# Block 2 projects the delta rule's keys and gates first, then the attention's queries and keys; the substitution is written between them

## The chip, the cores and the metric

The kernel runs on one core of one Trainium2 chip. The metric is device time in microseconds (us) of one execution; the time before is the median of three runs. A profile of one further execution tells what each engine did: TensorE (PE in the rows; PEld is its weight load), VectorE (DVE), ScalarE (ACT), GpSimd (POOL) and the queue that issues most transfers (SP).

## The reference

Two transformer blocks over one sequence of 512 tokens, 1024 channels, in float32. Block 1 (attention, pooling, a gated MLP) is not touched. Block 2 mixes tokens in two ways and then runs a mixture of experts:

```python
h = rms_norm(x, ln1_g)
proj = h @ w_in                      # 3*512 + 4*512 + 16 columns
aq, ak, av, dqkv, dz, dab = jnp.split(proj, ...)
aq = rms_norm(hs(aq), q_norm_g)      # 8 heads of 64
ak = rms_norm(hs(ak), k_norm_g)
attn = rms_norm(neighbourhood_attention(aq, ak, hs(av), rpb), attn_out_g)
dn = bidirectional_gated_deltanet(dqkv, dz, dab[:, :, 0], dab[:, :, 1], ...)
x = x + jnp.concatenate([attn, dn], axis=-1) @ w_out
x = x + hierarchical_moe(rms_norm(x, ln2_g), ...)
```

The delta net puts queries, keys and values through a convolution of width 5 and a SiLU, normalises queries and keys, and solves a unit lower triangular system per head, direction and chunk; its matrix is `beta * k k^T * decay`, so it needs the keys and the gates (from the 16 columns `dab`), but neither queries nor values:

```python
lower = jnp.where(strict, jnp.einsum('bhnid,bhnjd->bhnij', kb, k) * decay, 0.0)
a_mat = jnp.eye(c, dtype=f32) + lower
sol = lax.linalg.triangular_solve(a_mat, rhs, left_side=True, lower=True, unit_diagonal=True)
```

## The kernel before

Activations lie transposed, channels on partitions and the 512 tokens along the free dimension, in eight tiles. Every float32 product is made of three matmuls of rounded halves (`mm3`, lines 177 to 179): the weights are split by `split_w` into `whi` (ACT, line 170) and `wlo` (DVE, line 171) after their load into one of three `wraw` buffers, the activations into `hh` and `hl`.

Block 2's input is projected in chunks of 256 columns. `proj` makes 48 matmuls of 128x512 into two PSUM buffers `pj0` and `pj1`; the tag `mm` has two buffers, so a projection begins a buffer only when the last one's has been emptied. There are two chunks each of the attention's queries (`na_q`; in this text q0 and q1), its keys (k0, k1) and values (`na_v`; v0, v1), and of the delta rule's keys (`dn_k`), queries (`dn_q`), values (`dn_v`) and output gate (`dn_z`). `na_v` puts tokens on partitions: four groups of 24 matmuls 128x272 or 128x256 into one PSUM buffer each; v0 also has the 16 columns `dab` of the delta rule's gates. ACT empties these groups with a scale `rr` per token (line 792). `rr` is the reciprocal norm: column sums of the squares (line 311), a power on POOL (line 670), two products on DVE. The projections themselves run on unnormalised activations, and `RR`, its broadcast (line 351), is multiplied in by POOL at the convs (line 870).

`head_norm` follows q and k: ACT copies and squares the two PSUM buffers (lines 732 and 735), PE sums the squares (`hn`, 738), DVE scales (742, 743), POOL raises to the power -1/2 (745, two instructions on the tile `hnv`), DVE multiplies by `rr` (746). `head_rows` transposes the result on PE (`hr`, 753) and sends it through DRAM; `head_bcast` loads it back over partitions, and `na_q_out` and `na_k_out` multiply (772, 777; tiles `zq`, `akp`).

`conv_silu` follows the delta rule's q, k and v: ACT empties PSUM (869), POOL multiplies by `RR` (870), ACT starts and DVE adds four taps (871, 875), ACT makes the tanh (877), DVE the end (878). `gates` (900 to 928) makes the decays from `dab`. `dn_k_out` makes, per head, a transpose of the keys (`ktr`, 964), their square sums (968), `kk` = k k^T (984), and per direction the decay (`E`, 950 and 951) and `U` (990); one direction is transposed (996). Blocks of 32x32 of `U` go to DRAM (998) and come back as `LB` (1001), 128 blocks on 128 partitions. `substitute` inverts these blocks: for m from 31 to 1 a product (`TB`, 1019) and a sum (`XB`, 1021) over the columns above; DVE has columns 24 to 31 (31 steps), POOL those below 24 (23 steps). Its results go to DRAM (1025) and are used by `levels`, the stage behind the projections. `x_rows` (700) writes the normalised residual as rows, and the bias tables `bm` of the neighbourhood attention are made by POOL (812).

The order of work is not written engine by engine: except for one block of attention code with a schedule by hand, the framework's scheduler orders each engine's instructions when the program is built, from the written order, the dependencies and the number of buffers. Each engine then takes its instructions in that order. The written order of block 2's calls is what the change edits (lines 1211 to 1246, before).

Of the kernel before, what the change touches and what calls it, by code (L numbers as in the profile page):

```python
# [89 lines left out]
def hybrid_kernel(ctx, tc, A, out, dbg=None):  # L90
# [20 lines left out]
    def V(name, i=0, n=1):  # L111
        o, _ = _VEC[name]
        return vec[:, o + i:o + i + n]
# [42 lines left out]
    def split_w(src, n=8, into=None, w=256):  # L156

        his, los = [], []
        g = 1024 // w
        for k in range(0, n, g):  # L160
            m = min(g, n - k)

            def part(tag, dt):
                t = wp.tile([128, 1024], dt, tag=tag, name=tag, bufs=3)
                return t[:, :m * w].rearrange("p (m w) -> p m w", m=m)

            raw = into[k // 4] if into else part("wraw", F32)
            nc.sync.dma_start(raw, src[:, k:k + m, :])
            hi, lo = part("whi", F32R), part("wlo", F32R)
            nc.scalar.activation(hi, raw, AF.Copy)  # L170
            nc.vector.tensor_tensor(lo, raw, hi.bitcast(F32), op=ALU.subtract)  # L171
            his += [hi[:, i, :] for i in range(m)]
            los += [lo[:, i, :] for i in range(m)]
        return his, los
# [478 lines left out]

    w_first = split_w(A["win2"][0])
    nc.vector.tensor_tensor(gs[:, 8:16], V("fg", 0, 8), V("ln1", 0, 8), op=ALU.mult)
    hh, hl = new_h()
    for j in range(8):
# [66 lines left out]
    def head_norm(pp, gain):  # L726

        pt = ps("pa", "hn")
        aa = []
        for m in range(2):  # L730
            a = slot("cv", "a", 6)
            nc.scalar.activation(a, pp[m], AF.Copy, scale=gain)
            aa.append(a)
            sq = slot("cv", "sq", 6)
            nc.scalar.activation(sq, pp[m], AF.Square)
            for t in range(4):
                o = m * 8 + t * 2
                nc.tensor.matmul(pt[:, o:o + 2], sq[:, t * 128:t * 128 + 128], C("hsel"), start=True, stop=True)
        v, r = (sp_.tile([128, 2] + d, F32, tag=f"hn{i}", name="hnv", bufs=1 + i) for i, d in enumerate(([4, 2], [2, 4])))
        pv = pt[:, 0:16].rearrange("p (m t e) -> p m t e", m=2, t=4)  # L740
        for m in range(2):
            nc.vector.tensor_tensor(v[:, m], pv[:, m], rr2.unsqueeze(2).to_broadcast([128, 4, 2]), op=ALU.mult)
        nc.vector.tensor_scalar(v, v, 1.0 / 64, EPS, op0=ALU.mult, op1=ALU.add)
        for m in range(2):
            nc.gpsimd.tensor_tensor(v[:, m], v[:, m], nhalf.rearrange("p (t e) -> p t e", t=4), op=ALU.pow)
            nc.vector.tensor_tensor(r[:, m].rearrange("p e t -> p t e"), v[:, m], rr.unsqueeze(2).to_broadcast([128, 4, 2]),
                                    op=ALU.mult)
        return aa, r
# [15 lines left out]
        return R  # L764

    def na_q(c):
        return head_norm(proj(A["win2"][c] if c else w_first, hh, hl), g8)

    def na_q_out(c, aa, r):
        for m in range(2):  # L770
            R = head_bcast(r, m)
            nc.vector.tensor_tensor(unperm(zq[2 * c + m]), perm(aa[m]), perm(R), op=ALU.mult)
# [7 lines left out]

    def na_v(c):
        w = 256 if c else 272
        hi, lo = split_w(A["win2"][5] if c else A["win2v"], w=w)
        for i in range(4):
            p = ps("mm", "pv")
            ts = slice(i * 128, i * 128 + 128)
            for k in range(8):
                mm3(p[:, 0:w], hh[k][:, ts], hl[k][:, ts], hi[k], lo[k], k, k == 0, k == 7)
            if not c:
                nc.vector.tensor_scalar(dab[:, i, :], p[:, 256:272], rr[:, i:i + 1], None, op0=ALU.mult)  # L790
            v = slot("nP", "vn", 4, (128, 256))
            nc.scalar.activation(v, p[:, 0:256], AF.Copy, scale=rr[:, i:i + 1])
            nc.sync.dma_start(vscr[c][ts], v)
        src = vscr[c].rearrange("(r b x) w -> b r x w", r=8, b=8)
        for b in range(8):
            i, o = (b + 1) // 2, 64 * ((b + 1) % 2)
            nc.sync.dma_start(vsh[i][o:o + 64, c * 256:c * 256 + 256], src[b])
# [410 lines left out]
            new_mix2(4 + h)  # L1208
            split_h(mixh[4 + h], mixl[4 + h], da[h])

    q_ = na_q(0)
    x_rows(2)
    pk = proj(A["win2"][2], hh, hl)
    x_rows(0)
    k_ = head_norm(pk, V("kg"))
    q_ = head_rows(*q_)
    na_v(0)
    x_rows(3)
    x_rows(1)
    na_q_out(0, *q_)  # L1220
    rst.close()
    bp2 = st.enter_context(tc.tile_pool(name="blk2b", bufs=1))
    LB = slot("Z", "LB", 2, (128, 32, 32))
    XB = slot("Z", "XB", 2, (128, 32, 32))
    dn_k(0)
    gates()
    k_ = head_rows(*k_)
    dn_k(1)
    na_k_out(0, *k_)
    dn_k_out(0)  # L1230
    q2_ = na_q(1)
    pk2 = proj(A["win2"][3], hh, hl)
    dn_k_out(1)
    q2_ = head_rows(*q2_)
    na_q_out(1, *q2_)
    k2_ = head_norm(pk2, V("kg"))
    k2_ = head_rows(*k2_)
    na_k_out(1, *k2_)
    dn_q(1)
    dn_q(0)  # L1240
    na_v(1)
    substitute()
    dn_q_out(0)
    dn_v(1)
    dn_v(0)
# [679 lines left out]
```

## Time and profile before

| what | value |
|---|---|
| runs | 1555.94, 1557.53, 1548.36 us; median 1555.94 |
| profiled execution | 1553.21 us, span 1551.3 us |
| mean granted TensorE clock | 0.972 of full speed |
| instructions | 20448 |
| busy, share of the span | PE 95%, PEld 65%, DVE 54%, ACT 33%, POOL 16% |
| block 2's projections | about 613 to 845 us of the span |

The span runs from the first to the last instruction; the profiled execution's own time is 1.9 us above it. A row of the waits names what an engine waited for last; a timeline row gives start and duration, and in brackets the idle time of that engine just before it with what ended it. Matmuls are pipelined, so that the starts of two neighbours, and not the duration of one, give the rate. PEclk is the granted clock of TensorE, where 1.00 is its 2.4 GHz level and 0.50 the 1.2 GHz level.

### The profile page before, as it was taken

To read this page: it belongs to the slowest core of one execution; us is meant where nothing else is said; L and a number is where in the kernel's file an instruction comes from. 1 tells how busy PE (TensorE), PEld (TensorE's weight loads), DVE (VectorE), ACT (ScalarE), POOL (GpSimd) and SP (SyncE) were. 2 spreads that over 40 slices of the span, in tenths; PEclk is the share of its full clock that TensorE was granted. 3 is DMA by queue.
4 is the path that set the end of the run, shared out by engine and by line. 5 is a ranking of instruction groups with operands and counts; after the bars stand their busy time and mean duration, and the time that the engine had idled before them with its cause. 6 is when DMAs were issued, how large, how long until landed. Compare 5 with 4: busy or idle time off the path is not lost.

```text
span 1551.3 us, 20448 instructions
## 1 busy us (share of the span) xinstructions
PE 1467.0 (95%) x7500; PEld 1012.8 (65%) x7500; DVE 842.6 (54%) x1724; ACT 516.1 (33%) x981; POOL 251.6 (16%) x317
## 2 busy tenths in 40 slices
PE   6899999999999999998889999997999999999997
PEld 3766686888888887876667788884444444444443
DVE  3778776653564457266797666564333333233234
ACT  4554434441442345254334434422311111111111
POOL 0242021000000004323562330102100000000000
PEclk9989999999999999998989999997999999999999
DMA  8753143332222223353333131567999999999995
GB/s 334 244 201 122 60 145 109 103 101 94 96 96 95 95 82 99 101 171 102 85 116 77 30 92 50 196 220 295 421 418 424 425 423 424 424 424 424 423 424 185
DMA packets 82573, 327.69 MB, mean 211 GB/s; under 512 B 18086, under 2 KB 21798, under 8 KB 58144
## 3 DMA queue, kind: packets, MB, share of 16 engines
q1 hardware_dynamic: 80736, 321.63, 55.4%
q0 software_dynamic: 1728, 4.66, 0.8%
q8 instruction: 61, 1.00, 0.3%
q14 instruction: 48, 0.39, 0.1%
HBM read 319.42 MB, written 8.47 MB: 211 GB/s over the span
## 4 chain that ended last, share of the span: by engine, by line
PE 76%; DVE 10%; DMA 4%; issue 3%; POOL 3%; ACT 2%; SPq 1%; DVEq 0%; POOLq 0%; ACTq 0%
PE pgu L1728 14%; PE pj L177 10%; PE pj L179 10%; PE pj L178 10%; PE pd L1757 7%; PE pkept L1775 2%; PE pkept L1776 2%; PE pcmb L1775 2%; PE pcmb L1776 2%; DVE wlo L171 2%; DMA graw<-in_modw_dram 1%; DVE cv L875 1%; PE pS L485 1%; DMA xg<-xs,tok_of 1%; DVE E L950 1%
## 5 line engine op out<-in xcount | busy, mean ns | idle before, releaser
L177 PE MATMUL pj<-hh,whi 128*128 128x512 f32 x640 | 259.2, 406 | 16.1 <-ACT cn L869 7.7
L179 PE MATMUL pj<-hh,wlo 128*128 128x512 f32 x640 | 257.2, 403 | 4.8 <-DVE wlo L171 4.8
L178 PE MATMUL pj<-hl,whi 128*128 128x512 f32 x640 | 257.1, 402 | 0.5 <-DVE hl L200 0.5
L1728 PE MATMUL pgu<-wgu,xw 128*64 128x512 f32 x1024 | 227.1, 596 | 0.1
L171 DVE TENSOR_TENSOR wlo<-wraw,whi 128x1024 fp32r<-128x1024 f32 (+4 forms) x122 | 148.4, 1218 | 47.6 <-ACT whi L170 44.5
L170 ACT ACTIVATE whi<-wraw 128x1024 fp32r<-128x1024 f32 (+4 forms) x122 | 125.0, 1027 | 136.3 <-PE pj L178 119.2
L1728 PEld LDWEIGHTS pgu<-wgu,xw 128*64 128x64 f32 x1024 | 70.4, 137 | 139.3 <-issue 137.9
L177 PEld LDWEIGHTS pj<-hh,whi 128*128 128x128 f32 x640 | 123.5, 193 | 48.8 <-ACT cn L869 10.2
L179 PEld LDWEIGHTS pj<-hh,wlo 128*128 128x128 f32 x640 | 123.7, 194 | 34.6 <-DVE wlo L171 5.3
L178 PEld LDWEIGHTS pj<-hl,whi 128*128 128x128 f32 x640 | 123.8, 193 | 26.0 <-issue 1.2
L1734 DVE SCALAR_TENSOR_TENSOR hid<-pgu,agt,sg 128x256 f32<-128x256 f32 x32 | 15.5, 484 | 194.0 <-ACT sg L1732 194.0
L1732 ACT ACTIVATE sg<-pgu,agt 128x256 f32<-128x256 f32 x32 | 15.2, 476 | 305.1 <-PE pgu L1728 305.1
L1757 PE MATMUL pd<-wd,hT 128*64 128x512 f32 x512 | 115.5, 593 | 0.4 <-ACT xgT L1580 0.4
L1779 DVE TENSOR_TENSOR xr<-xr,pcmb 128x512 f32<-128x512 f32 x128 | 82.2, 683 | 28.7 <-PE pcmb L1776 28.7
L306 POOL TENSOR_TENSOR acc<-acc,sq 128x512 f32<-128x512 f32 x21 | 33.7, 1623 | 391.6 <-ACT sq L305 391.3
L198 DVE SCALAR_TENSOR_TENSOR og<-pd,agt,og 128x512 fp32r<-128x512 f32 x64 | 48.0, 750 | 79.6 <-ACT og L194 79.6
L1719 POOL COPY xw<-xgT 128x512 f32 x56 | 32.9, 616 | 353.8 <-PE pgu L1728 343.7
L1757 PEld LDWEIGHTS pd<-wd,hT 128*64 128x64 f32 x512 | 36.2, 137 | 72.3 <-issue 63.1
L179 PE MATMUL pj<-ah,wlo 128*128 128x512 f32 x176 | 69.3, 394 | 0.0
L177 PE MATMUL pj<-ah,whi 128*128 128x512 f32 x176 | 69.3, 394 | 0.0
L178 PE MATMUL pj<-al,whi 128*128 128x512 f32 x176 | 69.3, 394 | 0.0
L194 ACT ACTIVATE og<-pd,agt 128x512 fp32r<-128x512 f32 x64 | 44.0, 688 | 75.3 <-PE pd L1757 74.2
(455 smaller groups left out, 2630.3 us busy)
## 6 DMA issues: line engine op xcount, KB each, us to landing
wgu<-in_egu_dram SPq DMA_DIRECT2D x128, 1024.0 KB
wd<-in_ed_dram SPq DMA_DIRECT2D x62, 1024.0 KB
graw<-in_modw_dram SPq DMA_DIRECT2D x48, 512.0 KB
wraw<-in_wup_dram SPq DMA_DIRECT2D x42, 512.0 KB
wraw<-in_win_dram SPq DMA_DIRECT2D x38, 512.0 KB
wraw<-in_wdn_dram SPq DMA_DIRECT2D x20, 512.0 KB
wraw<-in_wout_dram SPq DMA_DIRECT2D x16, 512.0 KB
E<-gscr SPq DMA_DIRECT2D x16, 256.0 KB
```

The lines of the kernel that those rows point to most:

```text
L170: nc.scalar.activation(hi, raw, AF.Copy)
L171: nc.vector.tensor_tensor(lo, raw, hi.bitcast(F32), op=ALU.subtract)
L177: nc.tensor.matmul(p, whi, hh, start=first, stop=False)
L178: nc.tensor.matmul(p, whi, hl, start=False, stop=False)
L179: nc.tensor.matmul(p, wlo, hh, start=False, stop=last)
L194: nc.scalar.activation(hi, src, AF.Identity, scale=scale, bias=0.0 if bias is None else bias)
L198: nc.vector.scalar_tensor_tensor(lo, src, scale, hi.bitcast(F32), op0=ALU.mult, op1=ALU.subtract)
L1728: nc.tensor.matmul(gu[64 * i:64 * i + 64, :], xw[:, j, 64 * i:64 * i + 64], wts.gu[e][j], start=(j == 0), stop=(j == 7))
L1757: nc.tensor.matmul(pd[64 * i:64 * i + 64, :], hT[:, j, 64 * i:64 * i + 64], wts.d[e][:, j, n * 512:n * 512 + 512], start=(j == 0), stop=(j ...
L1775: nc.tensor.matmul(pc, OT[:, ts], a, start=(n == 1 or start), stop=False, skip_group_check=(n == 0))
L1776: nc.tensor.matmul(pc, OT[:, ts], b, start=False, stop=(n == 1 or stop), skip_group_check=(n == 0))
L1779: nc.vector.tensor_tensor(v, v, pc, op=ALU.add)
```

## The change

The calls of block 2 are written in another order; no instruction's work is altered. Values v0 with the gate columns come first (so the weights that are split while block 1 ends are `win2v`, not the first query chunk), then both halves of the delta rule's keys, the gates and `dn_k_out`, interleaved with q0 and k0, then q1 and k1. `substitute()` is written behind `head_rows` of q1, ahead of `head_norm` of k1, where it stood behind `dn_q` and v1. `na_v(1)` now stands ahead of `dn_q`.

```diff
-    w_first = split_w(A["win2"][0])
+    w_first = split_w(A["win2v"], w=272)
...
     def na_q(c):
-        return head_norm(proj(A["win2"][c] if c else w_first, hh, hl), g8)
+        return head_norm(proj(A["win2"][c], hh, hl), g8)
...
-        hi, lo = split_w(A["win2"][5] if c else A["win2v"], w=w)
+        hi, lo = split_w(A["win2"][5], w=w) if c else w_first
...
-    q_ = na_q(0)
+
+    na_v(0)
     x_rows(2)
-    pk = proj(A["win2"][2], hh, hl)
     x_rows(0)
-    k_ = head_norm(pk, V("kg"))
-    q_ = head_rows(*q_)
-    na_v(0)
+    dn_k(0)
     x_rows(3)
     x_rows(1)
-    na_q_out(0, *q_)
     rst.close()
     bp2 = st.enter_context(tc.tile_pool(name="blk2b", bufs=1))
     LB = slot("Z", "LB", 2, (128, 32, 32))
     XB = slot("Z", "XB", 2, (128, 32, 32))
-    dn_k(0)
     gates()
+    dn_k(1)
+    dn_k_out(0)
+    q_ = na_q(0)
+    dn_k_out(1)
+    pk = proj(A["win2"][2], hh, hl)
+    q_ = head_rows(*q_)
+    k_ = head_norm(pk, V("kg"))
+    na_q_out(0, *q_)
     k_ = head_rows(*k_)
-    dn_k(1)
+    q2_ = na_q(1)
     na_k_out(0, *k_)
-    dn_k_out(0)
-    q2_ = na_q(1)
     pk2 = proj(A["win2"][3], hh, hl)
-    dn_k_out(1)
     q2_ = head_rows(*q2_)
+    substitute()
     na_q_out(1, *q2_)
     k2_ = head_norm(pk2, V("kg"))
     k2_ = head_rows(*k2_)
     na_k_out(1, *k2_)
+    na_v(1)
     dn_q(1)
     dn_q(0)
-    na_v(1)
-    substitute()
     dn_q_out(0)
```

On POOL, before, the powers of the head norms of q1 (`hnv_5783`) and k1 (`hnv_6017`) stand among the work on the keys of the delta rule, and the first step of the substitution comes behind all of it (19 rows behind the first power):

```order
L745 TENSOR_TENSOR hnv_5783<-hnv_5783,nhalf_68 128x8 x2
L1011 MEMSET XB_5349 128x32
L973 TENSOR_TENSOR rk_4924<-ka_5652,nhalf_68 128x4
L745 TENSOR_TENSOR hnv_6017<-hnv_6017,nhalf_68 128x8 x2
L1090 MEMSET U_5675 32x4x32 x4
L1090 MEMSET U_5692 32x4x32 x4
L973 TENSOR_TENSOR rk_4924<-ka_5868,nhalf_68 128x4
L870 TENSOR_TENSOR cn_6103<-cn_6103,RR_4861 128x512
L1090 MEMSET U_5891 32x4x32 x3
```

After the change, POOL has the twelfth step (the last one with `12x12`) ahead of the power of q1's head norm, here `hnv_5907`:

```order
L1021 TENSOR_TENSOR XB_5243<-XB_5243,TB_5992 128x13x11
L1019 TENSOR_TENSOR TB_5992<-LB_5242,XB_5243 128x144
L1021 TENSOR_TENSOR XB_5243<-XB_5243,TB_5992 128x12x12
L745 TENSOR_TENSOR hnv_5907<-hnv_5907,nhalf_68 128x8 x2
L1019 TENSOR_TENSOR TB_5992<-LB_5242,XB_5243 128x143
L1021 TENSOR_TENSOR XB_5243<-XB_5243,TB_5992 128x11x13
```

and the last steps of the substitution ahead of that of k1's, here `hnv_6136`:

```order
L1021 TENSOR_TENSOR XB_5243<-XB_5243,TB_5992 128x2x22
L1019 TENSOR_TENSOR TB_5992<-LB_5242,XB_5243 128x23
L1021 TENSOR_TENSOR XB_5243<-XB_5243,TB_5992 128x23
L745 TENSOR_TENSOR hnv_6136<-hnv_6136,nhalf_68 128x8 x2
L870 TENSOR_TENSOR cn_6354<-cn_6354,RR_4867 128x512
L812 TENSOR_TENSOR bm_7185<-masks_4885,rb_7183 128x256
```

Both powers moved from ahead of the substitution's first step to behind its twelfth and its last.

On PE, before, the transpose `hr_5986` of q1's head norm follows the last matmuls of k1 (`pj1_5805`), and behind it come the square sums of k1 (`hn_6000`) and the delta rule's queries (`pj0_6052`):

```order
L178 MATMUL pj1_5805<-hl_4819,whi_5800 128x512
L179 MATMUL pj1_5805<-hh_4811,wlo_5801 128x512
L753 MATMUL hr_5986<-cst_64,hnv_5784 16x128
L738 MATMUL hn_6000<-cst2_4877,sq_6003 128x2 x4
L177 MATMUL pj0_6052<-hh_4804,whi_6042 128x512
L178 MATMUL pj0_6052<-hl_4812,whi_6042 128x512
```

After, it also follows k1 (`pj1_5937`), but reads `hnv_5908`, which DVE makes from POOL's `hnv_5907`; behind it stands v1 (`pv_6171`):

```order
L178 MATMUL pj1_5937<-hl_4825,whi_5932 128x512
L179 MATMUL pj1_5937<-hh_4817,wlo_5933 128x512
L753 MATMUL hr_5986<-cst_64,hnv_5908 16x128
L738 MATMUL hn_6119<-cst2_4883,sq_6122 128x2 x4
L177 MATMUL pv_6171<-whi_6161,hh_4810 128x256
L178 MATMUL pv_6171<-wlo_6162,hh_4810 128x256
L179 MATMUL pv_6171<-whi_6161,hl_4818 128x256
```

and 22 matmuls of v1 later the transpose `hr_6145` of k1's head norm, ahead of the rest of v1:

```order
L179 MATMUL pv_6171<-whi_6167,hl_4824 128x256
L177 MATMUL pv_6171<-whi_6167,hh_4817 128x256
L753 MATMUL hr_6145<-cst_64,hnv_6137 16x128
L178 MATMUL pv_6171<-wlo_6168,hh_4817 128x256
L179 MATMUL pv_6171<-whi_6167,hl_4825 128x256
L177 MATMUL pv_6199<-whi_6161,hh_4810 128x256
```

So the queue behind the first transpose is now v1 in place of the delta rule's queries, and the second transpose stands inside v1.

On DVE after the change the two products of line 746 (`hnv_5908`, which wait for POOL) stand between DVE's own steps of the substitution, and the low halves of v1's weights (`wlo_6162`) behind them:

```order
L742 TENSOR_TENSOR hnv_5907<-hn_5890,rr2_4853 128x8
L772 TENSOR_TENSOR zq_4892<-a_5571,hR_5818 128x8x8x8
L742 TENSOR_TENSOR hnv_5907<-hn_5890,rr2_4853 128x8
L1019 TENSOR_TENSOR TB_5992<-LB_5242,XB_5243 128x156
L743 TENSOR_SCALAR hnv_5907<-hnv_5907 128x16
L1021 TENSOR_TENSOR XB_5243<-XB_5243,TB_5992 128x26x6
L746 TENSOR_TENSOR hnv_5908<-hnv_5907,rr_4852 128x4x2 x2
L1019 TENSOR_TENSOR TB_5992<-LB_5242,XB_5243 128x175
L1021 TENSOR_TENSOR XB_5243<-XB_5243,TB_5992 128x25x7
L1019 TENSOR_TENSOR TB_5992<-LB_5242,XB_5243 128x192
L1021 TENSOR_TENSOR XB_5243<-XB_5243,TB_5992 128x24x8
L1019 TENSOR_TENSOR TB_5992<-LB_5242,XB_5243 128x184
L171 TENSOR_TENSOR wlo_6162<-wraw_6159,whi_6161 128x1024
```

In before the corresponding products stand ahead of the first step.

## Rows read from the trace of the kernel before

**Rows 1.** Head of the page: span, and each engine's busy time, share and instructions.

```profile
span 1551.3 us, 20448 instructions
...
PE 1467.0 (95%) x7500; PEld 1012.8 (65%) x7500; DVE 842.6 (54%) x1724; ACT 516.1 (33%) x981; POOL 251.6 (16%) x317
```

**Rows 2.** Table by stretches: us, length, busy us (count) of PE, PEld, DVE, ACT, POOL; PEclk, DMA, GB/s.

```profile
706.50:720.20 13.70, 11.32 (x37) 9.67 (x38) 8.05 (x22) 5.26 (x11) 5.04 (x11) 0.50 0.32 80
...
745.00:785.00 40.00, 30.62 (x174) 24.97 (x173) 32.03 (x72) 16.64 (x32) 24.61 (x48) 0.96 0.33 90
785.00:845.00 60.00, 53.13 (x237) 41.99 (x237) 50.87 (x116) 24.29 (x50) 22.78 (x31) 0.91 0.33 91
...
806.00:845.00 39.00, 35.80 (x171) 28.49 (x172) 30.63 (x68) 16.81 (x39) 7.94 (x8) 1.00 0.31 76
...
1060.00:1551.00 491.00, 479.97 (x2216) 218.29 (x2216) 170.30 (x281) 82.92 (x177) 42.65 (x66) 0.99 0.96 397
```

**Rows 3.** PE's waits from 600 to 860 us: us in total, times, longest us.

```profile
PE pj L177 <- ACT cn L869: 7.7, 5, 4.5
PE hn L738 <- ACT sq L735: 5.7, 2, 5.2
...
PE hr L753 <- DVE hnv L746: 1.6, 1, 1.6
```

**Rows 4.** Timeline of PE: start us, us, engine, line, operation, out<-in, count, idle before.

```profile
628.87 0.65 PE L351 MATMUL rb<-cst,rr 128*128 128x128 f32 x4
...
634.15 0.71 PE L700 MATMUL xtr<-cst,xT 128*128 128x128 f32 x5
...
649.79 0.37 PE L177 MATMUL pv<-whi,hh 128*128 128x272 f32 x1
...
663.99 1.04 PE L700 MATMUL xtr<-cst,xT 128*128 128x128 f32 x8
...
689.82 0.60 PE L964 MATMUL ktr<-cst,kT 128*128 128x128 f32 x4
...
708.88 1.87 PE L738 MATMUL hn<-cst,sq 128*128 128x2 f32 x8 [5.20 <-ACT sq L735]
...
745.44 0.50 PE L177 MATMUL pj<-hh,whi 128*128 128x512 f32 x1
...
806.24 0.50 PE L177 MATMUL pj<-hh,whi 128*128 128x512 f32 x1 [0.38 <-ACT cn L869]
...
844.42 0.60 PE L1058 MATMUL vtr<-cst,vT 128*128 128x128 f32 x4
```

**Rows 5.** Timeline of POOL, same columns.

```profile
691.87 3.99 POOL L812 TENSOR_TENSOR bm<-masks,rb 128x256 f32<-128x256 f32 x3
...
717.64 3.25 POOL L745 TENSOR_TENSOR hnv<-hnv,nhalf 128x8 f32<-128x8 f32 x2
...
766.93 0.24 POOL L1019 TENSOR_TENSOR TB<-LB,XB 128x23 f32<-128x23 f32 x1
...
771.56 0.40 POOL L1019 TENSOR_TENSOR TB<-LB,XB 128x95 f32<-128x95 f32 x1
...
782.70 0.81 POOL L1021 TENSOR_TENSOR XB<-XB,TB 128x144 f32<-128x144 f32 x1
...
791.79 1.22 POOL L1019 TENSOR_TENSOR TB<-LB,XB 128x95 f32<-128x95 f32 x1
...
797.51 0.24 POOL L1021 TENSOR_TENSOR XB<-XB,TB 128x23 f32<-128x23 f32 x1
```

**Rows 6.** Timelines of ACT, PE and DVE (twice), same columns.

```profile
707.13 0.63 ACT L951 ACTIVATE E<-E 128x512 f32<-128x512 f32 x1 [3.19 <-DVE E L950]
...
749.00 1.08 PE L984 MATMUL kk<-kT 128*128 128x128 f32 x8
...
760.07 0.70 DVE L996 STREAM_TRANSPOSE uT<-U 128x512 f32<-128x512 f32 x1
...
791.38 1.41 DVE L171 TENSOR_TENSOR wlo<-wraw,whi 128x1024 fp32r<-128x1024 f32 x1
```

## The prediction

> **What bounds the kernel now.** I read the head of the page first [rows 1]: TensorE (PE) is busy 1467.0 of 1551.3 us, so time is lost only where PE stops. The table by stretches [rows 2] shows where. From 1060 us on (the experts) PE is busy 479.97 of 491 us beside a DMA share of 0.96; that stage keeps its length and begins when block 2 ends, so a shift of block 2 passes whole to the span. In block 2's projections PE stops: busy 30.62 of 40 us from 745 to 785 and 53.13 of 60 from 785 to 845. PE's waits from 600 to 860 us [rows 3] name the releasers: evicted conv inputs (7.7 us), the squares of a head norm (5.7), a head norm's result (1.6). A stop also costs clock: after the 5.20 us stop at 703.68, 13.7 us run at a granted clock of 0.50 [rows 2, 4], the 1.2 GHz level, a loss of about 7 us.
>
> Milestones of before, from PE's timeline [rows 4]: q0 (queries, first half) done at 634.15, values v0 from 649.79 to 663.99, both halves of the delta rule's keys done at 689.82, then q1, k1 and the delta rule's second query half done at 745.44, last matmul of the stage's projections at 844.42 (the transposes of v follow). Price of one projection (48 matmuls): the last three take 806.24 to 844.42, 12.7 us each; without their idle time (39.00-35.80 = 3.2 us [rows 2]) 11.7. From 745.44 to 844.42 stand five projections and v1: 5 x 11.7 + 13 = 71.5 of 99 us (v1 by v0's 14.2 us with what is mixed into it, so 12 to 14). So 27 us are lost there, where conv, weight splits and substitution share VectorE (DVE).
>
> **The change, part by part.** Nothing is added or removed: the same instructions, in another order.
>
> *1. v0 first.* In before q0's matmuls need nothing of the normalisation; v0 has two PSUM buffers for four groups of 24 matmuls, and emptying one needs rr, which is there at about 628.9 (the rb matmul [rows 4]). So PE has only 48 matmuls of 14.2/96 = 0.15 us, 7 us, ahead of that wait, which is less than the 11.7 of q0. Then the other 48: from 629.5 some 7.5 us, end near 637, against q0's 634.15, of which 1 us is that v0 is the longer piece. The price is 1 to 3 us (ends 0 and 7).
>
> *2. Keys next.* From v0's end to the end of the second key half: 689.82-663.99 = 25.8 us, and 2 us for two more `x_rows` that now lie here: end at 637+28 = 665.
>
> *3. q0, k0, q1.* Three projections, where before ran q1, k1 and dn_q(1) in 745.44-689.82 = 55.6 us. That stretch held the 5.20 us stop and its half clock. The stop: ScalarE (ACT) held the squares behind an exp that had waited 3.19 us for DVE [rows 6], DVE was late with the conv, and the second conv input had waited on POOL behind three bias tables, 3.99 us [rows 5]. In the changed order these tables stand ahead of both. I take the stop at 2 us and half of the 7 us: 55.6-6.6 = 49, so q1 ends at T = 714 (ends 708 without any stop, 721 as before). In before the same set of work (v0 and five projections) is reached two projections ahead of 745.44, at 745.44-25.4 = 720. The new order is 6 us ahead at T (ends 12 and -1).
>
> *4. The substitution ahead of the head norms.* This is the part that costs. POOL takes its columns below 24: 23 steps. In the order rows the power of q1's head norm (hnv_5907) stands behind the first twelve steps, that of k1's (hnv_6136) behind the last eleven; in before both stand ahead of the first. Work from T:
> - The fourth head's `kk` comes soon after q1: T+1.5. In before, from that `kk` (749.00) to POOL's first step (766.93) it is 17.9 us, through square sums, decay, the transposed block at 760.07 and two transfers [rows 5, 6]. I take T+19 (the shortest sum of these rows' links gives 15).
> - Twelve steps, two instructions each: 766.93 to the end of `XB 128x144` at 783.51 is 16.6 us with a conv product among them, some 15.3 without it. A product of `128x95` took 0.40 us in one place and 1.22 in another [rows 5]; the steps at their shortest give about 11.2. I take 13: T+32. The two powers take 3.25, then DVE's two products and the transpose: PE is released at T+36.
> - PE meanwhile has k1 (11.7), two key blocks, the norm's sums and some 3 us of waits: it stands at `hr_5986` at T+20. **Stall 15 us** (ends 9.5 and 21). In before the same `hr` waited under 2 us. Behind it in PE's queue are k1's sums and all of v1; behind `hnv_5908` on DVE are v1's weight splits (`wlo_6162`, some 2 us later) and DVE's own steps.
> - Then 22 matmuls of v1, to T+43, and `hr_6145`, which needs the second power: POOL's eleven steps took 783.51 to 797.75, 14.2 us; I take 12 from T+35.5, then 3.25 and the products: T+52. **Stall 9 us** (ends 5 and 13).
> - The other 74 matmuls of v1, 9.5 us, and 3 us of half clock after two stops: T+64.5.
>
> At the contended step the row shows a POOL product of `128x95` taking 1.22 us from 791.79 while DVE ran a weight split of 1.41 us from 791.38 [rows 5, 6]. The Trainium skill (SBUF — State Buffer, section "Who interferes with whom") says that a DVE instruction with two SBUF inputs and a GpSimd instruction that reads SBUF exclude each other for a whole instruction. That agrees with this pair; and since DVE itself would stand waiting at `hnv_5908` for part of the twelve steps, by that rule they would run nearer to 11.2 us than to 15.3, and the sum would come out some 2 us below mine.
>
> *5. Six projections behind.* dn_q, dn_v, dn_z, twice each, with conv but hardly any substitution left on DVE: 6 x 12.3 (between 11.7 and 12.7) = 74. End at T+138.5 = 852.5, against 844.42: **8 us later**. The same as a difference: from T the changed order takes 138.5 us, the equal stretch of before took 844.4-720 = 124.4; 14 us lost behind T, 6 won ahead of it.
>
> *6. Queues.* No transfer is added. SP issues v1's weights and one more bias table's load earlier; the steps' scratch buffer takes one of three raw-weight buffers, as before. The levels' stage from 845 on gets its blocks of the substitution earlier than before, and in before it did not wait for them, so nothing is won there.
>
> The profiled execution took 1553.21 us (span 1551.3), the median of the runs is 1555.94. 1553.2 + 8 = 1561; carried to the median, 1555.9 + 8 = **1564 us**. About 1% (15.5 us) is what a measurement of this kernel can tell from no change.
>
> **Rivals.**
> *A. The stops do not shrink and the clock goes with them* (slower). If q1's squares wait as in before and v0 ends late (T = 721 or more) and each of the two stalls is followed by 13.7 us at 0.50 as after the stop at 703.68, that adds 7 for T and 7 to 11 of clock: end 22 to 26 us late, 1574 to 1582. For it: the 5.20 us stop was followed by just that. Against: a stop of 4.5 us on a conv input [rows 3] lies between 745 and 785, and there the mean clock was still 0.96 [rows 2].
> *B. The jam on DVE dissolves* (faster). If conv without substitution beside it lets the last six projections run at 11.0 each (8 us less), T falls at 708 (6 less) and the stalls are at their lower ends (9 less), the end comes 15 us early: 1541. By one mechanism: it decides at the point where POOL's first power is ready when PE gets to `hr_5986`; then 15 of the 24 us go, the sum is -7 and everything beyond comes from the projections. For this POOL would have to start 16 us earlier, at T+3, which the chain of 17.9 us from `kk` excludes unless the fourth head's keys get ahead of q1's matmuls; the order has `ktr_5654` behind them. Price 1537 to 1548.
> *C. Gain and stall cancel* (no change): both stalls at their lower ends and all else as forecast: 8-9 = -1 us, 1555, within 1%.
>
> **How the numbers follow.** The forecast (with ends 1557 to 1571) gets 0.50, A 0.27, C 0.12, B 0.11. From B only the part below 1540 counts as faster by over 1%, from the forecast the part above 1571.5 as slower, and I leave 0.10 for faster, since a shorter stall at both places would be enough to halve the sum: faster 0.10, same 0.63, slower 0.27. Low end 1546 (stalls -9, T -6, projections -3), high end 1582 (A).
>
> **What would show it.** In the changed profile: PE's wait at `hr` L753 on `hnv` L746 of 15 and 9 us, where 1.6 stood; POOL's powers (L745) directly behind `XB 128x144` and behind the last `XB 128x23`; DVE waiting for POOL at L746; v0's end near 637, q1's near 714; granted clock 0.50 behind the stalls; few waits from dn_q(1) on; the expert stage unchanged. I am wrong if L753's waits sum to under 12 us, if T lies outside 705 to 725, or if the levels begin earlier than 845.

## The result: 1567.35 us, 0.75% slower than before

| kernel | median of runs | lowest to highest | runs |
|---|---|---|---|
| before, beside it | 1554.60 us | 1548.36 to 1558.08 | 8 |
| changed | 1567.35 us | 1559.87 to 1569.96 | 8 |

The ratio of changed to before is 1.0075, with a 95% interval from 1.0058 to 1.0093. The forecast was 1564 us in a range from 1546 to 1582, and "same" by the 1% bound as the likeliest class; the medians differ by 12.75 us (0.8%).

Head of the page of the changed kernel; it answers to [rows 1]:

```profile
span 1568.0 us, 20450 instructions
...
PE 1473.8 (94%) x7500; PEld 1018.8 (65%) x7500; DVE 840.9 (54%) x1724; ACT 516.6 (33%) x981; POOL 246.1 (16%) x317
```

The work is the same (PE 7500 matmuls in both), and the span is 16.7 us longer. Three places make that up. Block 2's first matmul starts later, ahead of every call that the change moves; the stretch from there to the first matmul of the levels (`lvY`) is longer; and what is behind is 2.3 us longer. PE's timeline, of before:

```profile
616.77 0.47 PE L177 MATMUL pj<-hh,whi 128*128 128x512 f32 x1 [3.29 <-DVE xT L646]
...
844.86 1.06 PE L1098 MATMUL lvY<-DD,U 128*128 128x128 f32 x8
...
1064.33 2.21 PE L1728 MATMUL pgu<-wgu,xw 128*64 128x512 f32 x8
```

and of the changed kernel:

```profile
619.90 0.36 PE L177 MATMUL pv<-whi,hh 128*128 128x272 f32 x1 [2.87 <-DVE xT L646]
...
859.33 1.06 PE L1098 MATMUL lvY<-DD,U 128*128 128x128 f32 x8
...
1079.02 1.51 PE L1729 MATMUL pgu<-wgu,xw 128*64 128x512 f32 x6
```

So 619.90-616.77 = 3.1 us lie ahead of the change. The stretch was 844.86-616.77 = 228.1 us and is 859.33-619.90 = 239.4 us: **11.3 us are lost inside it**, most of the medians' 12.75 us. The work up to the first `lvY` is not quite equal: of the attention's small matmuls (`nS`, `nT`, `npo`) 26 stood ahead of it in before, 14 do now. To the first matmul of the experts (`pgu`), with all of block 2 ahead of it in both kernels, it is 1064.33-616.77 = 447.6 us and 1079.02-619.90 = 459.1 us, 11.5 us more. Over all the profiled executions below, the first matmul of block 2 began anywhere between 615.6 and 623.2 us, behind unaltered work, so the kernels are compared by this stretch as well as by their times.

PE's waits from 700 to 810 us in the changed kernel (columns as in [rows 3]: total, times, longest):

```profile
PE hn L738 <- ACT sq L735: 11.0, 3, 7.1
PE hr L753 <- DVE hnv L746: 5.2, 3, 2.3
PE hn L738 <- DVE hrow L755: 3.9, 1, 3.9
PE pv L178 <- DVE wlo L171: 2.4, 1, 2.4
```

and the table by stretches, in which the second and third row lie inside the first (columns as in [rows 2]):

```profile
723.30:783.00 59.70, 38.77 (x195) 33.90 (x196) 34.60 (x105) 14.09 (x28) 30.65 (x64) 0.71 0.36 102
733.80:750.90 17.10, 8.59 (x28) 7.44 (x29) 7.60 (x22) 3.52 (x5) 9.86 (x27) 0.50 0.50 135
757.70:774.80 17.10, 10.26 (x45) 9.68 (x46) 12.07 (x30) 2.60 (x4) 12.09 (x21) 0.50 0.30 94
783.00:852.90 69.90, 67.45 (x300) 52.47 (x298) 52.69 (x89) 30.60 (x55) 15.01 (x13) 1.00 0.31 88
```

In [rows 3] the conv inputs stood first with 7.7 us. Now the sums of a head norm (L738) do, with 11.0+3.9 us (over the 600 to 860 us of [rows 3] it is 11.6+3.9, and the conv inputs cost 6.0). From the end of q1 at 723.3 to the end of v1 PE is busy 38.8 of 59.7 us; two stretches of 17 us run at a granted clock of 0.50, the 1.2 GHz level, behind these stops. The six projections behind v1 are nearly free of stops: PE busy 67.45 of 69.9 us, where 785 to 845 had 53.13 of 60 [rows 2].

Where the 11.3 us lie is read at the end of k1. Up to there both kernels have projected the same seven pieces (v0, both key halves, q0, k0, q1, k1), and behind it the same other seven (v1 and six chunks of the delta rule). The two stretches, from the first matmul to the end of k1 and on to the end of the last projection, in before:

```profile
616.77:728.52 111.75, 103.06 (x519) 86.44 (x519) 58.78 (x129) 48.98 (x89) 36.35 (x43) 0.91 0.44 132
728.52:844.58 116.06, 97.70 (x483) 78.55 (x482) 90.44 (x216) 48.11 (x99) 54.05 (x89) 0.94 0.33 89
```

and in the changed kernel:

```profile
619.90:753.96 134.06, 113.00 (x542) 94.96 (x542) 70.65 (x192) 57.85 (x112) 50.46 (x92) 0.85 0.39 116
753.96:859.04 105.08, 93.41 (x446) 76.21 (x447) 77.06 (x148) 38.49 (x69) 30.60 (x39) 0.92 0.33 97
```

The changed kernel is **22.3 us late at the end of k1 and wins 11.0 us back behind it**. Of the 22.3 us, 12.4 are idle time of PE (21.1 us against 8.7). The rest is busy time: the mean granted clock is 0.85 against 0.91, and two more key heads' transposes and products, some 3 us, are done by then. Of the 11.0 us won back, 6.7 are idle time (11.7 us against 18.4).

### The profile page after: what moved, and what is told of

It is laid out like the page before. It is cut to its first block, busy times and chain, and to the rows that moved or that the text cites. A ratio compares the mean times of both kernels' runs of the same rounds, so it can differ in the third digit from the quotient of the medians.

```text
span 1568.0 us, 20450 instructions
## 1 busy us (share of the span) xinstructions
PE 1473.8 (94%) x7500; PEld 1018.8 (65%) x7500; DVE 840.9 (54%) x1724; ACT 516.6 (33%) x981; POOL 246.1 (16%) x317
## 4 chain that ended last, share of the span: by engine, by line
PE 76%; DVE 7%; DMA 7%; POOL 3%; issue 3%; ACT 2%; SPq 1%; DVEq 0%; ACTq 0%; POOLq 0%
PE pgu L1729 13%; PE pj L177 11%; PE pj L179 11%; PE pj L178 10%; PE pd L1758 7%; DMA graw<-in_modw_dram 3%; PE pkept L1776 2%; PE pkept L1777 2%; PE pcmb L1776 2%; PE pcmb L1777 2%; DMA xg<-xs,tok_of 1%; PE pS L485 1%; PE po L178 1%; PE po L177 1%; PE po L179 1%
## 5 line engine op out<-in xcount | busy, mean ns | idle before, releaser
L1733 ACT ACTIVATE sg<-pgu,agt 128x256 f32<-128x256 f32 x32 | 15.2, 476 | 304.8 <-PE pgu L1729 304.8
```

## Where PE stops now, and what is behind each stop

The timeline of PE in the changed kernel (start, duration, in brackets the idle time before and its releaser):

```profile
702.96 0.27 PE L753 MATMUL hr<-cst,hnv 128*16 128x128 f32 x1
...
715.03 0.28 PE L753 MATMUL hr<-cst,hnv 128*16 128x128 f32 x1 [0.95 <-DVE hnv L746]
...
735.22 1.87 PE L738 MATMUL hn<-cst,sq 128*128 128x2 f32 x8 [3.93 <-DVE hrow L755]
744.17 1.87 PE L738 MATMUL hn<-cst,sq 128*128 128x2 f32 x8 [7.09 <-ACT sq L735]
...
756.24 0.28 PE L753 MATMUL hr<-cst,hnv 128*16 128x128 f32 x1 [2.28 <-DVE hnv L746]
...
771.46 0.38 PE L753 MATMUL hr<-cst,hnv 128*16 128x128 f32 x1 [1.95 <-DVE hnv L746]
```

The first transpose, `hr` of q1's norm, which the prediction named as the place, waits 2.28 us at 756.24. The stop is one link earlier: 3.93+7.09 us at the sums (`hn`) of that same norm. Its cause is read backwards in the timelines of ACT and DVE:

```profile
743.52 0.60 ACT L735 ACTIVATE sq<-pj 128x512 f32<-128x512 f32 x1 [5.71 <-DVE zq L772]
...
734.29 0.71 DVE L996 STREAM_TRANSPOSE uT<-U 128x512 f32<-128x512 f32 x1
734.93 0.24 DVE L755 COPY hrow<-hr 16x128 f32<-16x128 f32 x1
738.41 0.28 DVE L755 COPY hrow<-hr 16x128 f32<-16x128 f32 x1 [3.24 <-DMA ublk<-uT]
...
742.66 0.83 DVE L772 TENSOR_TENSOR zq<-a,hR 128x512 f32<-128x512 f32 x1
...
754.17 0.17 DVE L746 TENSOR_TENSOR hnv<-hnv,rr 128x8 f32<-128x8 f32 x1 [6.27 <-POOL hnv L745]
```

ACT's square at 743.52 waited 5.71 us for DVE's product `zq` at 742.66: both use the six buffers `cv`, and the `a` that `zq` reads is what the square needs. `zq` needs `hR`, which comes through DRAM from `hrow`, and the two `hrow` copies, q0's and k0's, run at 734.93 and 738.41, though their transposes on PE are from 702.96 and 715.03. `hrow` and `hR` take their place in the four buffers `tmp`, which the decays `E` and the transposed blocks `uT` of the last key heads held; the second copy was released by a transfer out of `uT`. In before the fourth head's `kk` lay at 749.00 [rows 6], behind the transposes of all four head norms. There, too, the copies of q1 and k1 came behind the last `uT` (transposes at 728.36 and 738.10, copies at 760.70 and 770.79), but behind them stood no norm for which PE could have waited. In the changed order q0's and k0's rows stand behind the whole chain of the keys, and q1's squares stand behind these rows.

POOL's timeline of the changed kernel answers to [rows 5]:

```profile
740.52 0.23 POOL L1019 TENSOR_TENSOR TB<-LB,XB 128x23 f32<-128x23 f32 x1 [4.26 <-DMA LB<-ublk]
...
752.02 0.50 POOL L1021 TENSOR_TENSOR XB<-XB,TB 128x144 f32<-128x144 f32 x1
752.48 3.25 POOL L745 TENSOR_TENSOR hnv<-hnv,nhalf 128x8 f32<-128x8 f32 x2
...
758.91 1.27 POOL L1019 TENSOR_TENSOR TB<-LB,XB 128x128 f32<-128x128 f32 x1
```

The first step comes at 740.52, 17.3 us behind the end of q1. The twelve steps end at 752.52, 12.0 us later, and the power stands directly behind them, as the order had it. It does not wait for its operand, it begins as the steps end: POOL sets that moment. Its second half ends at 755.73, and PE, held up by the sums, has stood at `hr` for 1.8 us only. DVE waited 6.27 us for the first half (`hnv`, L746, in the rows above) with its own next step behind in its queue.

## Experiments

Each kernel ran beside the kernel before on the same chip. The stretch is that from block 2's first matmul to the first `lvY`, read from PE's timeline of one profiled execution; "stops" sums PE's idle times above 0.3 us in it. "To k1" and "to experts" are the times from the same first matmul to the end of k1 and to the first `pgu`. Differences of 2 or 3 us in these columns mean little: v0 alone took 18.7 to 21.5 us in the nine kernels that begin with it.

| kernel | median | ratio to before, 95% interval | to k1 | stretch | stops | to experts |
|---|---|---|---|---|---|---|
| before | 1553.8 to 1555.4 | 1 | 111.8 | 228.1 | 26.9 | 447.6 |
| changed | 1567.35 | 1.0075 [1.0058, 1.0093] | 134.1 | 239.4 | 32.3 | 459.1 |
| e1 substitution back at its old place | 1577.74 | 1.0148 [1.0107, 1.0188] | 130.3 | 248.7 | 39.6 | 469.4 |
| e2 before, substitution early | 1579.04 | 1.0157 [1.0129, 1.0184] | 109.9 | 245.8 | 43.4 | 469.3 |
| e3 q0 first | 1571.70 | 1.0112 [1.0084, 1.0139] | 136.7 | 242.3 | 42.1 | 461.3 |
| e4 substitution on POOL alone | 1588.39 | 1.0227 [1.0194, 1.0261] | 134.2 | 264.3 | 53.0 | 483.3 |
| e5 own buffers for hrow | 1574.94 | 1.0129 [1.0104, 1.0155] | 129.7 | 245.4 | 37.8 | 468.8 |
| e6 e1 and own buffers | 1576.27 | 1.0139 [1.0120, 1.0158] | 134.2 | 251.8 | 43.9 | 473.8 |
| e7 before, own buffers | 1562.03 | 1.0056 [1.0037, 1.0075] | 111.8 | 235.8 | 32.0 | 456.3 |
| e8 keys first, old order behind k1, own buffers | 1575.72 | 1.0130 [1.0103, 1.0157] | 133.6 | 246.3 | 43.9 | 469.0 |
| e9 no shared buffers in the norms | 1568.53 | 1.0110 [1.0072, 1.0148] | 115.4 | 233.5 | 26.4 | 456.7 |
| e10 powers on ScalarE | 1560.38 | 1.0052 [1.0031, 1.0072] | 132.5 | 229.6 | 25.8 | 451.0 |
| e11 e9 and e10 | 1571.40 | 1.0101 [1.0067, 1.0135] | 117.8 | 235.2 | 29.7 | 464.0 |
| e12 before, no shared buffers | 1555.59 | 1.0006 [0.9985, 1.0027] | 110.9 | 224.1 | 26.5 | 443.9 |

The column "to k1" tells the kernels apart. With the delta rule's keys behind k0, as in before, k1 ends at 109.9 to 111.8 us (before, e2, e7, e12). With the keys ahead of k0 it ends at 129.7 to 136.7 us, wherever q0, the substitution, v0 or v1 stand, except in e9 and e11, whose norms share no buffers: 115.4 and 117.8 us. So the late k1 comes from the keys' place together with the shared buffers and the order that follows from them.

### One part at a time: e1, e2, e3

e1 moves one call of the changed kernel back:

```diff
     q2_ = head_rows(*q2_)
-    substitute()
     na_q_out(1, *q2_)
...
     dn_q(1)
     dn_q(0)
+    substitute()
     dn_q_out(0)
```

> The changed kernel with one part undone: the substitution is written at its old place, behind both query halves of the delta rule; keys, gates and v0 stay first and v1 stays ahead of the delta rule's queries. Queue theory (the loss comes from the substitution's steps standing ahead of head-norm work in the in-order queues of DVE and POOL): the stops of PE between the end of q1 and the end of v1 (21 us in the changed kernel, at L738, L753, L178) fall under 7 us, the two 17 us stretches at half clock shrink to one of at most 10, and the time is 12 to 20 us below the changed kernel, 1548 to 1555 us, so no slower than before. Start theory (the loss comes from v0 and the keys being first; the substitution's place is innocent): 1562 to 1570 us as the changed kernel.

Measured: 1577.74 us, outside both. Waits of PE from 600 to 880 us:

```profile
PE pj L177 <- ACT cn L869: 18.2, 4, 14.2
PE hn L738 <- ACT sq L735: 8.9, 3, 6.7
PE hn L738 <- DVE hrow L755: 5.8, 1, 5.8
```

and on POOL the substitution's first and last step and the row behind it:

```profile
770.44 0.62 POOL L1019 TENSOR_TENSOR TB<-LB,XB 128x23 f32<-128x23 f32 x1 [12.41 <-DVE wlo L171]
...
794.62 0.23 POOL L1021 TENSOR_TENSOR XB<-XB,TB 128x23 f32<-128x23 f32 x1
794.81 1.26 POOL L870 TENSOR_TENSOR cn<-cn,RR 128x512 f32<-128x512 f32 x1
```

With the substitution away, the stops at the sums stay (6.7+5.8 us), so **the substitution does not make them**. POOL's 23 steps hold it from 770.44 to 794.85, 24.4 us, and the conv product of the delta rule's first query half stands behind: PE stops 14.2 us for it. In the changed order the early place is the better one, by 10 us. Up to the end of k1 both take about as long (130.3 and 134.1 us); from there to the end of the last projection e1 takes 118.2 us, nearly as before with 116.0, and the changed kernel 105.1. So the loss comes with the new order of what is written up to k1, as the start theory had it (e1 is slower than its range, too), and the substitution's early place is what wins time back. That part of its steps then lies under a stop that is there anyway is my reading, not shown.

e2 makes the opposite move alone, in the kernel before: `substitute()` behind `head_rows` of q1.

> The kernel before with one part of the change alone: the substitution is written behind the head rows of q1, the rest as before. Queue theory: PE stops at the head norm of q1 and k1 (L738, L753) appear, 10 to 20 us in sum where 7 stood, and the time is 6 to 18 us above before, 1561 to 1573 us. Start theory: within 4 us of before, 1551 to 1559 us.

Measured: 1579.04 us, 25 us above before, 6 us more than the queue theory's upper end. PE's waits from 700 to 810 us:

```profile
PE nS L815 <- DVE hrow L755: 9.0, 2, 6.7
PE pj L177 <- ACT whi L170: 7.3, 1, 7.3
PE ktr L964 <- DVE U L990: 6.9, 1, 6.9
```

The stops come where nothing of the substitution is named: the attention's first logits (`nS`) wait for `hrow`, the last key head for `U`, a weight half for its load. One call moved and the scheduler ordered the logits ahead of projections. `hrow` again stands behind the last `uT` (at 755.69, the copies at 756.33 and 759.94). So each part alone costs more than the two together (24 and 25 us against 12.75): they don't add up.

e3 projects q0 ahead of v0:

```diff
-    w_first = split_w(A["win2v"], w=272)
+    w_first = split_w(A["win2"][0])
...
-    na_v(0)
+    q_ = na_q(0)
     x_rows(2)
+    na_v(0)
...
     dn_k_out(0)
-    q_ = na_q(0)
     dn_k_out(1)
```

> The changed kernel with another part undone: q0 is projected first (its weights are the ones split early), v0 behind it, then the keys. Queue theory: the start gives back 1 to 4 us at most and the stops behind q1 stay at 15 to 24 us: 1562 to 1568 us. Start theory: the loss is gone, 1552 to 1558 us.

Measured: 1571.70 us, above both ranges. With q0 first nothing is given back, and 10.3+7.8 us stay at the sums (L738), so v0's place is not the cause. The keys stay ahead of k0 and q1 here, so e3 does not test that part of the start theory; the column "to k1" and e8 below bear on it.

### What holds the sums: e4, e5, e6, e7, e9

e4 gives POOL all columns of the substitution, so that DVE's queue has none of its steps:

```diff
-            for eng, t0, c0, c1 in ((nc.vector, 0, max(m, 24), 32), (nc.gpsimd, 512, m, 24)):
+            for eng, t0, c0, c1 in ((nc.vector, 0, 32, 32), (nc.gpsimd, 0, m, 32)):
```

> The changed kernel with all columns of the substitution on POOL, none on DVE. If it is DVE's queue that holds up PE (the products zq behind DVE's first steps keep the buffers that the squares of q1's norm need), the 7.1 us stop at L738 falls under 3 us; POOL's steps are longer then, so the stop at L753 grows from 2.3 us to 5 to 12 us, and the time stays within 6 us of the changed kernel, 1561 to 1573. If neither queue matters, the stops at L738 and L753 stay as in the changed kernel.

Measured: 1588.39 us. PE's waits from 700 to 810 us:

```profile
PE hr L753 <- DVE hnv L746: 20.6, 3, 15.1
PE hn L738 <- ACT sq L735: 10.5, 3, 7.4
...
PE hn L738 <- DVE hrow L755: 3.5, 1, 3.5
```

The stop at the sums stays (7.4 and 3.5), so DVE's steps ahead of `zq` are not its cause, against my expectation. The stop at the second `hr` grows from 1.95 to 15.1 us, as the queue theory says of longer steps, and more than I had allowed.

e5 takes `hrow` out of `tmp`:

```diff
-        row = tmp("hrow")[0:16, 0:128]
+        row = (slot("rw", "hrow", 2, (128, 128)) if bp2 else tmp("hrow"))[0:16, 0:128]
```

> The changed kernel with one resource added: the 16x128 tile hrow (the copy of a head norm's transpose, L755 of before) has two small buffers of its own instead of one of the four 128x512 buffers tmp, which the decays E, the transposed blocks uT and hR share. Buffer theory (the 11 us stop of PE at the sums of q1's norm, L738, comes from q0's and k0's hrow copies waiting until E and uT of the last key heads have left tmp): that stop falls under 3 us. Buffer theory alone gives 1553 to 1560 us. With the queue theory beside it (POOL's steps hold k1's power, so PE stops at the second transpose instead, 10 to 20 us where 1.95 stood) the time is 1561 to 1569 us. If tmp is not the cause, the stop at the sums stays at 8 to 12 us.

Measured: 1574.94 us. PE's waits from 700 to 810 us (the line numbers are two higher here), and the rows of DVE and ACT ahead of the stop:

```profile
PE hr L755 <- DVE hnv L748: 14.6, 2, 11.8
PE hn L740 <- ACT sq L737: 10.9, 2, 9.3
...
735.99 0.69 DVE L774 TENSOR_TENSOR zq<-a,hR 128x512 f32<-128x512 f32 x1 [5.27 <-DMA hR<-hscr]
...
736.72 0.60 ACT L737 ACTIVATE sq<-pj 128x512 f32<-128x512 f32 x1 [7.91 <-DVE zq L774]
```

The stop shrinks from 11.0 to 9.3 us only: the square waits 7.9 us for `zq`, and `zq` now 5.3 us for `hR`, the other tile in `tmp`. And the stop at the second `hr`, behind POOL's steps, is 11.8 us where 1.95 stood: what PE no longer loses at one it loses at the other, as the second reading of the expectation had it. The time missed that reading's range by 6 us.

e6 puts the same buffers into e1.

> The same own buffers for hrow, in the kernel with the substitution at its old place (e1_late). Buffer theory: the 12.5 us stop at L738 falls under 3 us, the 14 us stop at the conv input behind POOL's steps stays (8 to 16 us): 1562 to 1570 us against 1577.7. If tmp is not the cause: 1574 to 1581.

Measured: 1576.27 us, as e1 and within the last reading: the stop at the sums was 15.2 us and that at the conv input 14.2. Own buffers for `hrow` alone do not remove the stop at the sums.

e7 is the control in before.

> Control: own buffers for hrow in the kernel before (for the three head norms written after the second pool opens). If before also waits on tmp there, 3 to 8 us faster, 1546 to 1551; if the four buffers only bind where the keys' chain is written ahead of the head rows, within 4 us: 1550 to 1558.

Measured: 1562.03 us, 8 us slower, outside both ranges. Two small buffers changed the order that the scheduler chose, and a stop of 8.4 us at a conv input appeared. A buffer is not a neutral probe here.

e9 replaces every shared buffer of the norms, on top of e5:

```diff
-            sq = slot("cv", "sq", 6)
+            sq = vR[2 + m]
...
-        R = tmp("hR")
+        R = vR[m]
```

> The changed kernel with every shared buffer of the head norms replaced: hrow in two small buffers of its own, hR and the squares sq in the four tiles vR, which nothing uses until the values are transposed. Own buffers for hrow alone moved the stop of PE at the sums of q1's norm one link on: ScalarE's square waited 7.9 us for the product zq, which waited for hR behind the transposed block uT. Buffer theory: that stop (11.0 us in the changed kernel, 9.3 with own hrow) falls under 3 us, the head norms finish ahead of the substitution's first step, and PE's next stop is at v1's weights or the dn_q conv behind the steps, 4 to 12 us; time 1554 to 1564 us. If the stop is not from buffers, it stays at 8 to 12 us and the time at 1564 to 1575.

Measured: 1568.53 us, as the changed kernel. PE's waits from 700 to 810 us:

```profile
PE hr L755 <- DVE hnv L748: 5.6, 2, 4.1
PE pv L178 <- DVE wlo L171: 5.2, 2, 3.1
PE pv L177 <- ACT whi L170: 3.6, 1, 3.6
...
PE hn L740 <- ACT vR L737: 1.7, 2, 1.2
...
750.76 1.47 DVE L171 TENSOR_TENSOR wlo<-wraw,whi 128x1024 fp32r<-128x1024 f32 x1
```

The stop at the sums is gone (1.7 us in two), and k1 ends at 115.4 us where it was 134.1. So its cause is shown: the shared buffers, with the order that the scheduler makes from them (three tiles were replaced at once). But the gain does not last. The head norms' powers and DVE's first eight steps now stand ahead of v1's weight split, which DVE reaches at 750.76, and PE stops at `hr`, at v1's high halves and at its low halves, 14 us in sum. At the end of v1 this profile is 12.3 us ahead of the changed kernel's (149.9 us from the first matmul against 162.2), at the first `lvY` 5.9 and at the experts 2.4. In the levels and behind them PE waits 2.5, 2.1, 1.6 and 2.0 us for four tiles of these stages (`sr`, `NX`, `za`, `kT`), where the changed kernel has 0.6, 0.4, 0.3 and 0.5. What makes these waits longer was not tried.

### What POOL's queue costs: e10, e11, e12

```diff
-            nc.gpsimd.tensor_tensor(v[:, m], v[:, m], nhalf.rearrange("p (t e) -> p t e", t=4), op=ALU.pow)
+            nc.scalar.activation(v[:, m], v[:, m], AF.Ln)
+            nc.scalar.activation(v[:, m], v[:, m], AF.Exp, scale=-0.5)
```

> The changed kernel with the head norms' power on ScalarE, as exp(-0.5 ln v), instead of on POOL (two instructions more per half, the result differs in the last digits). Queue theory of the prediction (PE waits at hr for POOL's power behind the substitution's steps): the stops at L753 of before (2.3 and 2.0 us) go, and as the 11 us stop at the sums of q1's norm stays, the gain is 3 to 8 us at most: 1560 to 1565. If POOL's queue costs the 24 us that the prediction's stalls gave it, 1545 to 1552. If POOL is not concerned at all: 1566 to 1572.

Measured: 1560.38 us. PE's waits from 700 to 810 us:

```profile
PE hn L738 <- ACT sq L735: 10.0, 2, 6.9
PE hn L738 <- DVE hrow L756: 3.6, 1, 3.6
PE hr L754 <- DVE hnv L747: 1.4, 2, 1.2
```

Nothing is left at the second `hr`, nothing at v1's low halves, and the stops at the sums are as they were. The stretch is 229.6 us, 9.8 less, of which 1.6 lie in v0, ahead of anything that the edit touches; to the experts it is 8.1 less. The stops of the stretch fall by 6.5 us, and those that stood open behind the sums in the changed kernel were 2.28+2.38+1.95 = 6.6. The medians' distance to before falls from 12.75 to 5.0 us; by the ratios it falls from 0.75 to 0.52%, 3.6 us, and their intervals overlap. POOL's queue is thus worth some 4 to 8 of the 12 us, with the larger end by the trace.

e11 joins e9 and e10.

> Both: no shared buffers for the head norms and the power on ScalarE. If buffers and POOL's queue are two covers over the same time, this run gives more than the two single gains together, 1545 to 1555 us, and could beat before; if they are independent, the sum of the single gains; if neither is the cause, 1564 to 1572.

Measured: 1571.40 us, the third reading's time, though each of the two is shown above to stop PE. With the buffers apart, the order is that of e9, in which the powers stand ahead of the steps anyway and v1's weights are what is late (5.6 and 3.5 us); there the move to ScalarE has nothing to give. To the experts e11 takes 7.3 us more than e9, 5.6 of them behind the stretch; why is open.

e12 is the control of e9 in before.

> Control: the same buffers in the kernel before. If its 5.2 us stop at the sums of q1's norm (squares behind an exp on ScalarE) is not from buffers, it stays and the time is within 8 us of before, 1550 to 1562 (own hrow alone was 8 us slower there); if it is, 1542 to 1549.

Measured: 1555.59 us, no change (its profile is 3.7 us shorter to the experts, but block 2 began 5.6 us later in it). The 5.2 us stop at the sums fell to 0.8, and 4.6 us at the key transposes and 3.1 us at the square sums of the queries came in its place.

e8 took the keys-first head and the order of before behind k1.

> Keys and v0 first as in the changed kernel, own buffers for hrow, and behind k1 the order of before (both query halves of the delta rule, then v1, then the substitution). If the head (keys first) is worth the 6 us that the prediction gave it once the stop at L738 is gone, the time is 1545 to 1551, below before; if POOL's steps only move to another place, 1555 to 1566.

Measured: 1575.72 us, outside both ranges; stops of 13.1 us at the sums and 7.2 and 4.7 at conv inputs. k1 ends at 133.6 us although all behind it stands as in before, so the late k1 comes with the head, as in e1. No kernel was faster than before.

## Why the prediction was right, and where it was not

Counted from block 2's first matmul, forecast against the changed kernel's timeline:

| step | forecast | measured |
|---|---|---|
| 1. v0 done | 20.2 us | 641.24-619.90 = 21.3 |
| 2. both key halves, from there | 28 | 671.5-641.2 = 30.3 |
| 3. q0, k0, q1, from there | 49 | 723.3-671.5 = 51.8 |
| T, from the first matmul | 97.2 | 723.26-619.90 = 103.4 |
| 4. POOL's first step, from T | 19 | 740.52-723.26 = 17.3 |
| twelve steps | 13 | 12.0 |
| PE released at the first `hr`, from T | 36 | 756.24-723.26 = 33.0 |
| PE at the first `hr`, from T | 20 | 753.96-723.26 = 30.7 |
| **stall at the first `hr`** | 15 | **2.3** |
| stall at the second `hr` | 9 | 1.95; with two stops ahead of it 2.38+2.63+1.95 = 7.0 |
| v1 done, from T | 64.5 | 781.9-723.3 = 58.6 |
| 5. six projections | 74 | 858.9-781.9 = 77.0 |
| sum against before | +8 | +11.3 |

**Right**: the sign, the size to 4 us, POOL's timing to 3 us, the half clock behind the stops, the undisturbed projections behind v1, and the stage behind block 2, which passed the shift on. The likeliest class, within 1%, holds. That the sum came so near is in part luck. Counted from the first matmul, its three terms were off by +6.2 us (T), -5.9 (from T to the end of v1) and +3.0 (the six projections), which leaves +3.3.

**Wrong in step 3**: "the new order is 6 us ahead at T". The 720 us for before came from taking two undisturbed projections, 25.4 us, off 745.44. But k1 and dn_q(1) took 41.8 us there: q1 ends at 703.68, where the 5.20 us stop [rows 4] begins, and the stop and its half clock lie behind it. So before reached the same set of work at 703.68-616.77 = 86.9 us, and the changed kernel, with T at 103.4, is 16.5 us behind there. Stops at conv inputs (2.71 and 2.66 us) and at sums and transposes took the place of the one that shrank, v0 ran at half clock for much of its time (granted clock 0.68 from 619.90 to 641.20), and two key heads' products lie ahead of T.

**Wrong in what costs**: step 4 calls the substitution ahead of the head norms "the part that costs", and step 5 counts 14 us lost behind T. Behind T the changed kernel takes 135.8 us to the end of the last projection and before 140.9, so 5 us are won there. By e1 the early place is worth some 10 us, and by e1, e8 and the column "to k1" the loss comes with the keys ahead of the norms.

**Wrong in step 4's stall**: the stall of 15 us "at `hr`". By the test that the prediction set itself (waits at L753 under 12 us in sum) that step fell: they sum to 5.2. PE came to `hr` 11 us late, because it had stopped at the sums of the same norm, where I had put "some 3 us of waits". I had read the order of POOL's queue and missed the buffers: in before, too, the first `hrow` copy stands at 760.70, right behind the `uT` of [rows 6], and I did not ask what held it up. e5 and e9 show that chain. e5 and e4 show that POOL's steps can hold PE as forecast: with the norms' rows freed in part, or with longer steps, 11.8 and 15.1 us stand at the second `hr`; and e10 shows what that queue costs in the changed kernel itself, 4 to 8 us, not 24. The two waits do not add up because they lie over the same time: in this order the power begins as POOL's twelfth step ends, so PE could not be released before T+33.0, whichever wait it spent until then. And the work from T to the end of v1 had been counted 6 us too long: 58.6 us less the stops (21.0) and the clock (9.4, below) is 28.2, where the forecast's 64.5 less its stalls, waits and clock (30) left 34.5. That error and the shorter stops (21.0 us for 27) hid the two others, in step 3 and in the clock.

Of the shared access that stood beside step 4: POOL's product took 1.27 us at 758.91 beside DVE's weight split of 1.48 us from 758.44, and from 748.29 on, while DVE waited at L746, the steps of 128x135 to 128x144 took 0.44 to 0.50 each. The Trainium skill (SBUF — State Buffer, section "Who interferes with whom") says that a VectorE instruction with two inputs in SBUF contends with a GpSimd instruction that reads SBUF, and that whichever has their shared ports keeps them for a whole instruction; by it the twelve steps were to be nearer 11.2 than 15.3 us, and they took 12.0. That DVE's standing still made them short is not shown: beside DVE's own steps of the substitution, from 755.70 to 758.84, POOL's steps of 128x135 to 128x143 took 0.42 to 0.52 as well.

**Rivals.** A (slower) had two of its parts right: T came later, and behind each group of stops 17 us ran at half clock, with 8.59 and 10.26 us of busy time in them, a loss of about 9.4 us (half of that) where the forecast had 3. It ended short of A's 22 us since the stops were 21.0 us and not 27. Of B (faster) the projections did run almost without stops, but they took 77.0 us, not 66, and not less than the forecast's 74. C did not happen.

**What stays open.** Why removing the stop at the sums gives so little back in the end (18.7 us at the end of k1, 2.4 at the experts, nothing in the median) is read from e9's waits, not proved: every removal also changed the order on several engines. What the sums' stop would be worth in an otherwise equal order was not tried, since the scheduler sets the order anew with each buffer.

## What to carry to other kernels

When a call is written earlier, ask of each engine's queue what now stands behind it, and of each rotating buffer what must leave it first; a copy of 0.24 us that shares buffers with a long chain waits for the chain. Stops that lie over the same time don't add up: find the moment that releases the engine last, and count from it; removing the stop ahead of it can only make the next one longer, as in e5. Where a scheduler sets the order, each probe is a new order, so read what moved before what it cost. And take the point at which two orders are compared from the row where the same work ends, not from prices taken off another row.

## What was not expected

Two buffers of 512 bytes per partition cost the kernel before 8 us (e7, ratio 1.0056 [1.0037, 1.0075]), by the new order as far as the rows show. Moving the norms' two powers (3.25 us together on POOL) to four instructions on ScalarE was the only edit that brought the changed kernel's median down (e10).
